# Sample attention beside GDN's chain: ScalarE copies every turned page out of PSUM, in place of taking turns with VectorE

## Chip, cores and metric

One core of a Trainium2 chip runs the whole kernel. The metric is the device time of one execution in microseconds (us); lower is better. The kernel before takes 1189.36 us in the median of three runs (1189.23 to 1190.71).

## The reference, cut to what matters

The reference is one inference step of a decoder layer for two groups that share all weights: a prompt of 16 meta tokens and 512 tokens, and a sample group of 8 sequences with 8 new tokens each. A token-mixing block runs two branches on one input projection: differential attention, and a gated DeltaNet (GDN). Then come gates, an output projection and a gated ConvFFN. The change touches the sample group's attention over its cache: each of the 8 sequences has 2048 cached keys in 16 pages of 128 tokens, found through a page table.

```python
k_past = cache_k[l][page_table].reshape(ds, -1, DA_HEADS, 2, DA_HEAD_DIM)
v_past = cache_v[l][page_table].reshape(ds, -1, DA_HEADS, 2 * DA_HEAD_DIM)
s_past = jnp.einsum('bqhmd,bkhmd->bhmqk', qs, k_past)
s_new = jnp.einsum('bqhmd,bkhmd->bhmqk', qs, k)
pr = jax.nn.softmax(jnp.concatenate([s_past, s_new], axis=-1), axis=-1)
a = pr[:, :, 0] - lam * pr[:, :, 1]
out = einsum('bhqk,bkhe->bqhe', a[..., :n_past], v_past) + einsum(..., a[..., n_past:], v)
```

GDN, which runs beside it, solves a triangular system per chunk of 128 tokens and carries a state from chunk to chunk; it does so for four heads, one after the other.

## The kernel before, in words

**Two streams.** Lines 228 to 247 merge two generators into one program. The main stream does the prompt's attention and then, from `self.chain = True` on (line 232), the four GDN heads (`gdn_chain`, line 711). The stream beside it does the sample attention (line 1353) and then 16 gate projections. While the chain flag is set the main stream has right of way, and the other stream is recorded wherever the main stream asks for a delay. A scheduler below that lays the instructions out in one fixed order on each engine when the program is built, so an edit to one operation can move others.

**Sample attention** takes the sequences in four pairs. A page of keys arrives by DMA from SP's queue as `page` (a tile holds two pages; five tiles rotate). TensorE turns it: four transposes of 128x128, one per head (line 419), into one PSUM bank `ps_t` (three banks rotate). The bank is copied into `KT` (line 1403, 128x512); then TensorE multiplies `KT` by the queries into the bank `ps_s` (one bank), from which VectorE makes the masked scores `S` and their maxima (line 1235). A `KT` tile holds two pages, j = 0 and j = 1: VectorE copies j = 0 and ScalarE copies j = 1. There are 64 `KT` tiles in all, 16 to a pair. After the softmax the pages of values are multiplied without being turned.

**GDN's chain.** Per head, three convolutions (lines 647 and 649 on VectorE, 653 on ScalarE) give q, k and v; two Gram products follow, and then a solve of the 16x16 blocks, `gdn_base` (line 936): row sums (969, 970), a first step (971), and 14 steps of shuffle, multiply and subtract (975 to 977) that run on VectorE alone, one after the other. Their end is `xyt` and `xy` (981, 987), which TensorE transposes to go on. Products that widen the solved blocks follow, and the chunk-by-chunk state (875 to 909). Between these TensorE does wide projection products into `ps_d` (for `z`, the next head's q, k and v, and gates); their weights are loaded as `wraw` (line 309), rounded by ScalarE into `whi` (313), and VectorE subtracts to get `wlo` (314).

Of the kernel before, what the change touches and what calls it, by code (L numbers as in the profile page):

```python
# [150 lines left out]
class Body:  # L151
# [1201 lines left out]
    def sample_attention(self, pool):  # L1353
        nc, a = self.nc, self.a
# [23 lines left out]
        def pages(cache, ids):  # L1378

            t = self.t(pool, [128, 2, 512], "page", bufs=5)  # L1380
            for k, i in enumerate(ids):
                tag, value = entry(cache, i)
                move = nc.sync.dma_start(t[:, k], cache[bass.ds(value, 1)].rearrange("o t e -> (o t) e"))
                moves[tag] = move.ins
            return t

        for pr in range(NB // 2):
# [4 lines left out]
            for g in range(4):  # L1392
                sp = self.ps("s")
                for u in range(2):
                    kts = []
                    for e in range(2):
                        kp = pages(ck, [(2 * pr + e) * NPG + 4 * g + 2 * u + j for j in range(2)])
                        kt = self.t(pool, [128, H, 256], "KT", bufs=4)
                        for j in range(2):
                            tp = self.ps4("t")  # L1400
                            for h in range(H):
                                self.transpose(tp[:, h], kp[:, j, 128 * h : 128 * h + 128])
                            (nc.scalar.copy if j % 2 else nc.vector.tensor_copy)(kt[:, :, 128 * j : 128 * j + 128], tp)  # L1403
                        kts.append(kt)
                    yield DELAY[26]
                    for e, kt in reversed(list(enumerate(kts))):
                        for h in range(H):
                            self.mm(
                                sp[32 * h : 32 * h + 32, 256 * u : 256 * u + 256], self.qb[:, 2 * pr + e, h], kt[:, h],
                                start=e == 1, stop=e == 0,  # L1410
                            )
                    yield 0.0
                self.score(S[:, 512 * g : 512 * g + 512], sp, self.zeros(512), -3e38, mx[:, g : g + 1])
# [16 lines left out]
            tp = self.ps("t")  # L1430
# [9 lines left out]
            for g in range(4):  # L1440
                tp = self.ps4("t")
# [24 lines left out]
            if pr % 2:  # L1466
                self.head_norm(pool, os)
                yield DELAY[30]
                tp = self.ps("t")
# [722 lines left out]
```

## Time and profile before

| | value |
|---|---|
| median of 3 runs | 1189.36 us |
| the profiled execution | 1191.39 us, of which the span from first to last instruction is 1189.6 us |
| TensorE's mean granted clock | 0.983 |
| TensorE busy | 1136.4 us, 96% |
| VectorE busy | 734.6 us, 62% |
| ScalarE busy | 512.1 us, 43% |

Times in rows are microseconds from the span's start unless they are marked ns. PE is TensorE, PEld its weight loads, DVE VectorE, ACT ScalarE, POOL GpSimd, and SPq SyncE's queue of DMA issues. An idle time in square brackets is that of the engine just before the row, with what ended it.

### The profile page before, as it was taken

Reading aid. Unit: us, or ns where it says so; the run is one execution under the profiler, and the core shown is the slowest. Engines: PE = TensorE matmul, PEld = TensorE weight load, DVE = VectorE, ACT = ScalarE, POOL = GpSimd, SP = SyncE. Lnnn points to the kernel's source line nnn. Section 1 sums busy time; section 2 is a strip of 40 time slices with the busy share of each in tenths; the row PEclk is TensorE's granted clock in tenths of the full one; section 3 lists DMA queues with packets and bytes.
Section 4 is the critical chain, followed back from the end, with each engine's and each line's share of the span. In section 5 each row is a group of like instructions: output and inputs, shape, how many; then the busy total and the mean of one; then the engine's idle time right before and its main releaser. Section 6 shows DMA issues by size and latency. Waiting matters only on the chain.

```text
span 1189.6 us, 23613 instructions
## 1 busy us (share of the span) xinstructions
PE 1136.4 (96%) x8683; PEld 1014.2 (85%) x8683; DVE 734.6 (62%) x1877; ACT 512.1 (43%) x1242; POOL 283.1 (24%) x390
## 2 busy tenths in 40 slices
PE   6999999988999998999999999999999999999997
PEld 5987787766677777779999897789999999999996
DVE  5446657578389368446333874479889889842323
ACT  5235545443253343324232534445565565832321
POOL 2122221041242223213010001434554544300000
PEclk9999999998999999999999999989999999999999
DMA  6374434835857674742323346323333332432322
GB/s 201 79 242 137 134 86 131 272 112 173 275 164 232 215 249 145 231 125 55 89 55 83 88 124 188 114 73 105 100 91 95 103 89 82 136 98 74 103 74 80
DMA packets 184348, 157.56 MB, mean 132 GB/s; under 512 B 12571, under 2 KB 146274, under 8 KB 184232
## 3 DMA queue, kind: packets, MB, share of 16 engines
q1 hardware_dynamic: 179713, 147.53, 41.2%
q0 software_dynamic: 3264, 5.16, 1.4%
q10 hardware_dynamic: 1254, 3.35, 0.9%
q8 instruction: 69, 1.13, 0.4%
q14 instruction: 48, 0.39, 0.1%
HBM read 146.12 MB, written 9.88 MB: 131 GB/s over the span
## 4 chain that ended last, share of the span: by engine, by line
PE 71%; issue 13%; DVE 8%; POOL 3%; ACT 3%; DMA 1%; SPq 0%; DVEq 0%; POOLq 0%; ACTq 0%
PE ps_d L271 26%; PE ps_t L271 17%; PE ps_g L271 14%; PE ps_s L271 6%; PE ps_t L419 6%; PE ps_m L271 1%; DVE cy L649 1%; DVE KT L1403 1%; DMA page<-in_cache_v 1%; DVE vt L656 1%; POOL grr L786 1%; POOL r L383 0%; POOL dbig_up L749 0%; POOL hss L383 0%; DMA x<-in_x_prompt 0%
## 5 line engine op out<-in xcount | busy, mean ns | idle before, releaser
L271 PE MATMUL ps_d<-xhi,whi 128*128 128x256 f32 (+2 forms) x704 | 219.8, 313 | 0.0
L314 DVE TENSOR_TENSOR wlo<-wraw,whi 128x512 fp32r<-128x512 f32 x196 | 138.4, 721 | 127.7 <-ACT whi L313 126.0
L271 PE MATMUL ps_d<-xhi,wlo 128*128 128x256 f32 (+2 forms) x704 | 213.9, 304 | 0.6 <-DVE wlo L314 0.6
L271 PE MATMUL ps_d<-xlo,whi 128*128 128x256 f32 (+2 forms) x704 | 213.9, 304 | 0.3 <-DVE xlo L314 0.2
L313 ACT CAST whi<-wraw 128x512 fp32r<-128x512 f32 (+1 forms) x198 | 117.0, 611 | 165.4 <-PE ps_d L271 94.1
L271 PEld LDWEIGHTS ps_d<-xhi,whi 128*128 128x128 f32 x704 | 134.8, 192 | 7.8 <-issue 4.6
L271 PEld LDWEIGHTS ps_d<-xlo,whi 128*128 128x128 f32 x704 | 134.8, 192 | 3.6 <-issue 2.5
L271 PEld LDWEIGHTS ps_d<-xhi,wlo 128*128 128x128 f32 x704 | 134.5, 191 | 1.9 <-DVE wlo L314 1.0
L419 PE MATMUL ps_t<-consts,page 128*128 128x128 f32 x512 | 73.5, 283 | 7.7 <-DVE KT L1403 6.5
L419 PEld LDWEIGHTS ps_t<-consts,page 128*128 128x128 f32 x512 | 57.5, 143 | 24.4 <-issue 10.3
L271 PE MATMUL ps_t<-fhit,hw 128*128 128x290 f32 x228 | 68.0, 298 | 0.0
L271 PE MATMUL ps_t<-flot,hw 128*128 128x290 f32 x228 | 67.7, 297 | 0.0
L271 PE MATMUL ps_t<-fhit,lw 128*128 128x290 f32 x228 | 67.6, 297 | 0.0
L1403 ACT COPY KT<-ps_t 128x512 f32<-128x512 f32 x64 | 37.4, 585 | 65.4 <-PE ps_t L419 63.0
L313 ACT CAST hw<-sw 128x512 fp32r<-128x512 f32 x76 | 47.2, 623 | 40.6 <-PE ps_t L271 19.8
L314 DVE TENSOR_TENSOR lw<-sw,hw 128x512 fp32r<-128x512 f32 x76 | 59.4, 782 | 8.1 <-ACT hw L313 8.1
L1403 DVE COPY KT<-ps_t 128x512 f32<-128x512 f32 x64 | 43.7, 684 | 19.0 <-PE ps_t L419 18.8
L271 PEld LDWEIGHTS ps_t<-flot,hw 128*128 128x128 f32 x228 | 43.2, 190 | 0.0
L271 PEld LDWEIGHTS ps_t<-fhit,lw 128*128 128x128 f32 x228 | 43.1, 189 | 0.0
L271 PEld LDWEIGHTS ps_t<-fhit,hw 128*128 128x128 f32 x228 | 43.0, 189 | 0.0
L271 PE MATMUL ps_s<-KT,qb 128*32 128x256 f32 x512 | 38.1, 402 | 1.4 <-DVE KT L1403 1.1
L1870 DVE SCALAR_TENSOR_TENSOR fy<-fpre,fw,fy 128x592 f32<-128x592 f32 x44 | 36.5, 828 | 0.9 <-ACT fy L1868 0.2
(683 smaller groups left out, 3073.8 us busy)
## 6 DMA issues: line engine op xcount, KB each, us to landing
page<-in_cache_k SPq DMA_DIRECT2D x128, 256.0 KB, 4.3
page<-in_cache_v SPq DMA_DIRECT2D x128, 256.0 KB, 4.5
wraw<-in_w_in SPq DMA_DIRECT2D x88, 256.0 KB, 3.0
wraw<-in_w_ffn_in SPq DMA_DIRECT2D x50, 256.0 KB, 3.0
wraw<-in_w_down SPq DMA_DIRECT2D x40, 256.0 KB, 3.5
raw<-in_w_ffn_in SPq DMA_DIRECT2D x38, 256.0 KB, 2.9
wraw<-in_w_out SPq DMA_DIRECT2D x16, 256.0 KB
x<-in_x_prompt SPq DMA_DIRECT2D x4, 512.0 KB, 8.6
```

Of the source, the lines that this page charges most:

```text
L271: return self.nc.tensor.matmul(out, lhsT, rhs, **kw).ins
L313: self.nc.scalar.copy(hi, raw)
L314: (eng or self.nc.vector).tensor_tensor(out=lo, in0=raw, in1=hi.bitcast(F32), op=ALU.subtract)
L419: self.nc.tensor.transpose(out, in_, self.ident[:k, :k])
L649: nc.vector.scalar_tensor_tensor(out=y, in0=pre[:, j : j + n], scalar=self.cw[:, ch, 24 + j : 25 + j], in1=y, op0=ALU.mult, op1=ALU.add)
L656: nc.vector.scalar_tensor_tensor(out=dst, in0=part(th), scalar=1.0, in1=part(y_), op0=ALU.add, op1=ALU.mult)
L786: nc.gpsimd.tensor_tensor(out=rr, in0=rr, in1=self.mhalf[:, :10].rearrange("p (a b) -> p a b", a=2), op=ALU.pow)
L1403: (nc.scalar.copy if j % 2 else nc.vector.tensor_copy)(kt[:, :, 128 * j : 128 * j + 128], tp)
L1870: nc.vector.scalar_tensor_tensor(out=y, in0=pre[:, j : j + 592], scalar=fw[:, m, 16 + j : 17 + j], in1=y, op0=ALU.mult, op1=ALU.add)
```

## The change

Pages that are recorded while the chain flag is set are copied by ScalarE for both j; before that the two engines go on taking turns.

```diff
                             for h in range(H):
                                 self.transpose(tp[:, h], kp[:, j, 128 * h : 128 * h + 128])
-                            (nc.scalar.copy if j % 2 else nc.vector.tensor_copy)(kt[:, :, 128 * j : 128 * j + 128], tp)
+                            copy = nc.scalar.copy if j or self.chain else nc.vector.tensor_copy
+                            copy(kt[:, :, 128 * j : 128 * j + 128], tp)
                         kts.append(kt)
```

Of the 64 copies on VectorE 42 move to ScalarE: 10 of the second pair, which is under way when the chain starts, and 16 each of the third and the fourth. A new line shifts later line numbers by one. The scheduler then lays the engines out differently from there on, in three places above all.

TensorE while it turns pages beside the first head's solve, before (`page` and `KT` are the sample group's keys, `ps_d` the wide products, here for `z`):

```order
1183 L419 MATMUL ps_t_3723<-consts_66,page_3710 128x128 x4
1184 L271 MATMUL ps_d_4435<-xhi_6_85,whi_4428 128x256
1185 L271 MATMUL ps_d_4435<-xlo_7_86,whi_4428 128x256
1186 L419 MATMUL ps_t_3729<-consts_66,page_3710 128x128 x4
1187 L271 MATMUL ps_d_4462<-xhi_8_87,whi_4428 128x322
1188 L271 MATMUL ps_d_4462<-xlo_9_88,whi_4428 128x322
1189 L419 MATMUL ps_t_3747<-consts_66,page_3743 128x128 x4
```

And the same pages now:

```order
1182 L419 MATMUL ps_t_3723<-consts_66,page_3710 128x128 x4
1183 L419 MATMUL ps_t_3729<-consts_66,page_3710 128x128 x4
1184 L419 MATMUL ps_t_3747<-consts_66,page_3743 128x128 x4
1185 L419 MATMUL ps_t_3753<-consts_66,page_3743 128x128 x2
1186 L271 MATMUL ps_s_3684<-KT_3722,qb_304 32x256 x4
```

The wide products no longer stand between the pages. From the transposes of `kn` to the transpose of `xyt` TensorE's order had 49, 44 and 44 of them in the three solves with pages beside them; now it has 15, 2 and 15, and the others stand behind `xyt`. Eight score products moved behind it as well in the second and in the third of these solves.

VectorE in the first head's solve, before:

```order
538 L971 TENSOR_TENSOR xc_3617<-xc_3617,lc_3615 128x5
539 L1403 COPY KT_3697<-ps_t_3698 128x4x128
540 L975 STREAM_SHUFFLE row_3628<-xc_3617 128x5x2
541 L1403 COPY KT_3722<-ps_t_3723 128x4x128
542 L976 TENSOR_TENSOR row_3628<-row_3628,lc_3615 128x5x2
543 L1403 COPY KT_3746<-ps_t_3747 128x4x128
544 L977 TENSOR_TENSOR xc_3617<-xc_3617,row_3628 128x5x2
```

And now:

```order
536 L971 TENSOR_TENSOR xc_3617<-xc_3617,lc_3615 128x5
537 L314 TENSOR_TENSOR wlo_4429<-wraw_4424,whi_4428 128x512
538 L975 STREAM_SHUFFLE row_3628<-xc_3617 128x5x2
539 L314 TENSOR_TENSOR wlo_4432<-wraw_4426,whi_4428 128x512
540 L976 TENSOR_TENSOR row_3628<-row_3628,lc_3615 128x5x2
541 L314 TENSOR_TENSOR wlo_4513<-wraw_4508,whi_4512 128x512
542 L977 TENSOR_TENSOR xc_3617<-xc_3617,row_3628 128x5x2
```

The page copies are gone from between the steps; the weight subtractions, which stood a few steps further on, moved up into their places.

SP's queue of loads, before, where the next head's weights `wraw_4637` to `wraw_4749` are asked for (`page` from `in_cache_v` are pages of values):

```order
298 L1383 DMA page_4018<-in_cache_v 128x512
299 L309 DMA wraw_4510<-in_w_in 128x4x128
300 L309 DMA wraw_4637<-in_w_in 128x4x128
301 L309 DMA wraw_4639<-in_w_in 128x4x128
302 L309 DMA wraw_4747<-in_w_in 128x4x128
303 L309 DMA wraw_4749<-in_w_in 128x4x128
```

And now:

```order
365 L1383 DMA page_4390<-in_cache_k 128x512
366 L720 DMA st_4499<-in_state_gdn 128x8x128
367 L309 DMA wraw_4637<-in_w_in 128x4x128
368 L309 DMA wraw_4639<-in_w_in 128x4x128
369 L309 DMA wraw_4747<-in_w_in 128x4x128
```

Those loads moved back past all pages of values of this pair, four tiles of the next pair's keys and the next head's state.

## Rows read from the trace of the kernel before

**Rows 1.** The page: busy time, share of the span, instructions.
```profile
PE 1136.4 (96%) x8683; PEld 1014.2 (85%) x8683; DVE 734.6 (62%) x1877; ACT 512.1 (43%) x1242; POOL 283.1 (24%) x390
```

**Rows 2.** Stretches: PE, PEld, DVE, ACT, POOL busy (count), PEclk, DMA share, GB/s.
```profile
255.00:265.00 10.00, 7.99 (x55) 5.45 (x54) 5.88 (x20) 3.84 (x10) 3.43 (x4) 0.83 0.08 23
265.00:275.00 10.00, 6.40 (x56) 4.90 (x54) 9.88 (x20) 2.73 (x5) 5.37 (x6) 0.88 0.61 189
275.00:285.00 10.00, 9.93 (x88) 6.66 (x86) 7.44 (x31) 2.35 (x4) 1.12 (x2) 0.78 0.56 161
```

**Rows 3.** TensorE's waits, 235 to 545 us: in total, times, longest.
```profile
PE ps_t L419 <- DVE KT L1403: 6.9, 5, 3.2
...
PE ps_t L419 <- ACT KT L1403: 2.1, 3, 1.4
...
PE ps_t L419 <- DVE tailT L639: 1.2, 1, 1.2
```

**Rows 4.** Line 1403 by engine, whole span: ns min/median/max, first and last start.
```profile
L1403 DVE COPY KT<-ps_t x64: 669/684/692, 65.1 to 475.9; 128x512 f32<-128x512 f32 x64
L1403 ACT COPY KT<-ps_t x64: 564/586/604, 65.9 to 476.2; 128x512 f32<-128x512 f32 x64
```

**Rows 5.** Line 1403 in the three solves: DVE and ACT busy (count), PEclk, DMA.
```profile
255.00:295.00 40.00, 6.83 (x10) 5.87 (x10) 0.87 0.51 153
355.00:387.00 32.00, 8.18 (x12) 7.02 (x12) 1.00 0.71 219
451.00:483.00 32.00, 6.82 (x10) 5.88 (x10) 0.95 0.64 198
```

**Rows 6.** TensorE in order of time, around the three solves: start, length, instruction, [idle].
```profile
258.21 0.29 PE L419 MATMUL ps_t<-consts,kn 80*128 80x80 f32 x1 [2.01 <-DVE kn L793]
...
274.20 1.11 PE L419 MATMUL ps_t<-consts,page 128*128 128x128 f32 x4 [3.22 <-DVE KT L1403]
...
293.41 0.27 PE L419 MATMUL ps_t<-consts,xyt 80*80 80x80 f32 x1
...
355.44 0.68 PE L419 MATMUL ps_t<-consts,kn 80*128 80x80 f32 x5
356.05 1.07 PE L271 MATMUL ps_s<-KT,qb 128*32 128x256 f32 x16
357.05 1.53 PE L419 MATMUL ps_t<-consts,page 128*128 128x128 f32 x12
...
386.02 0.27 PE L419 MATMUL ps_t<-consts,xyt 80*80 80x80 f32 x1
...
451.16 0.67 PE L419 MATMUL ps_t<-consts,kn 80*128 80x80 f32 x5
...
482.53 0.27 PE L419 MATMUL ps_t<-consts,xyt 80*80 80x80 f32 x1
```

**Rows 7.** VectorE in order of time, first solve.
```profile
262.78 0.69 DVE L1403 COPY KT<-ps_t 128x512 f32<-128x512 f32 x1 [2.27 <-PE ps_t L419]
263.39 0.85 DVE L649 SCALAR_TENSOR_TENSOR cy<-pre,cw,cy 128x616 f32<-128x616 f32 x1
...
272.71 0.83 DVE L971 TENSOR_TENSOR xc<-xc,lc 128x5 f32<-128x5 f32 x1
...
278.26 0.69 DVE L1403 COPY KT<-ps_t 128x512 f32<-128x512 f32 x1 [1.21 <-PE ps_t L419]
...
293.12 0.24 DVE L981 TENSOR_TENSOR xyt<-xc,consts 80x80 f32<-80x80 f32 x1
```

**Rows 8.** ScalarE in order of time, first solve.
```profile
275.40 0.59 ACT L1403 COPY KT<-ps_t 128x512 f32<-128x512 f32 x1 [5.13 <-PE ps_t L419]
```

**Rows 9.** Stretch with wide products alone: PE busy (count), PEclk, DMA share, GB/s.
```profile
290.00:293.00 3.00, 3.00 (x22) 1.00 1.02 298
```

**Rows 10.** What SP's queue waited for, 225 to 560 us: in total, times, longest.
```profile
SPq L720 <- DMA out_new_gdn_sample<-st: 8.6, 2, 7.0
```

**Rows 11.** The tile `wraw`, 225 to 560 us: from issue to landing.
```profile
DMA to landing us min/median/max: 3.0/3.9/4.8
```

## The prediction

> **What bounds the kernel now.** I read the page first. TensorE is busy for 96% of the span, VectorE for 62%, ScalarE for 43% [rows 1]. So what counts is TensorE's idle time and its clock; moving work between the other two engines pays only where TensorE waits for one of them. Over the whole span a VectorE with 38% to spare says nothing of that, so the next view is the table of stretches. Around the first head's solve it shows what the averages hide: from 265 to 275 us VectorE is busy for 9.88 of 10 us and TensorE for only 6.40, and ScalarE for 2.73 [rows 2]. In this stretch VectorE is the bound and ScalarE is free. The clock is part of it: the granted clock is 0.83, 0.88 and 0.78 in three slices of 10 us [rows 2], so 3.4, 2.4 and 4.4 us of them passed at 1.2 instead of 2.4 GHz, each after TensorE had waited.
>
> The list of waits says for whom. Between 235 and 545 us TensorE waits 6.9 us for page copies on VectorE, 2.1 us for those on ScalarE and 1.2 us for another late VectorE copy, `tailT` [rows 3]. The longest, 3.22 us, ends at 274.20 [rows 6]; ScalarE meanwhile had been idle for 5.13 us because no turned page came [rows 8]. The page sat in PSUM behind a queue of GDN work on VectorE. That is 10.2 us in the three rows, the size of the prize. The trace in order of time shows who is late next: the solve on VectorE runs from 272.71 to the `xyt` at 293.12 [rows 7], and TensorE takes `xyt` up at 293.41 [rows 6] at once. It had wide products to do until then.
>
> **What the change moves.** 42 copies leave VectorE, 42 x 0.684 = 28.7 us, and 42 x 0.586 = 24.6 us come to ScalarE [rows 4]. Neither sum is on TensorE's path as such. I therefore work out each of the three solves with pages beside them, from TensorE's `kn` to its `xyt`: how much earlier VectorE delivers, less the TensorE work that the new order puts off until after `xyt`. That work isn't saved, only done later, and it has to be paid from the same 96%.
>
> *First solve:* 35.2 us now, 258.21 to 293.41 [rows 6]. Ten VectorE copies leave it [rows 5], at 0.61 us from one start to the next, 262.78 to 263.39 [rows 7]: 6.1 us. Two waits of VectorE for turned pages, 2.27 and 1.21 us [rows 7], go with them, as far as nothing else (the Gram products, which TensorE does after the same pages) is late then. Bounds 6.1 and 9.6 us; I take 8.3, near the upper one, since the copy that waited 1.21 us stood inside the chain of steps, where nothing takes its place. Put off: 49 - 15 = 34 wide products. A stretch with such products alone does 22 in 3.00 us [rows 9], 0.136 us each: 4.6 us. Gain 8.3 - 4.6 = 3.7 us, between 1.5 and 5.0. TensorE itself, without its wait for copies and with part of the half clock gone, would be at `xyt` 2 to 4 us before VectorE: the wait for pages turns into a shorter wait for the solve.
>
> *Second solve:* 30.6 us now, 355.44 to 386.02 [rows 6], at full clock [rows 5]. Twelve copies go, 7.3 us; one weight subtraction moves in, about 0.6 us as any VectorE pass over 128x512. 6.7 us earlier. Put off: 44 - 2 = 42 wide products, 5.7 us, and eight score products, which are the 16 matmuls of a row of 1.07 us [rows 6]: 6.8 us. Gain 0, between -1.5 and +1.
>
> *Third solve:* 31.4 us now, 451.16 to 482.53 [rows 6]. Ten copies, 6.1 us; put off 29 x 0.136 = 3.9 and again 1.1 us. Gain 1.1, between 0 and 2.5.
>
> *Where the third and the fourth pair of sequences start,* outside of the solves: the 1.2 us for `tailT` and the longest wait for a ScalarE copy, 1.4 us [rows 3]. Both were late because VectorE was: the second stood in ScalarE's order behind a SiLU of a convolution that VectorE had not finished. Four and six VectorE copies leave there. 2.6 us; bounds 0 and 3.4.
>
> *What it costs.* A pair of pages that two engines copied side by side in 0.68 us takes ScalarE 2 x 0.586 = 1.17 us [rows 4]. TensorE needs 2 x 0.51 us to turn them (twelve transposes in 1.53 us make three pages) and half of 1.07 us for their scores [rows 6], 1.55 us together. So ScalarE keeps up on average with a quarter to spare; that is the cover, and it is gone where several pages are turned without scores between them, as the new order does more often. GDN's own small copies on ScalarE queue behind pages too. I take 1 us; bounds 0 and 10.2 (21 pairs x 0.49 us, each on the path). The Trainium skill, "TensorEngine Tiling (Array Packing)", section "PSUM Bottleneck", speaks against this change: use both ScalarE and VectorE to empty PSUM. By it the cost is the upper bound, and the sum would come out 9.2 us later; by the row, TensorE's 1.55 us hide it.
>
> *After the new waits* for `xyt` the clock may fall again, as it did after the old ones. Such a slice lost half of 4.4 us, 2.2 us [rows 2]. Two solves have such a wait; I take 1.5 us, between 0 and 4.4.
>
> *DMAs:* the next head's weight loads stand behind the pages of values, keys and the state on SP's queue. They now follow a state load that waited up to 7.0 us for a store [rows 10], and land 3.0 to 4.8 us after issue [rows 11]. In TensorE's new order 32 page transposes and 38 wide products stand between the state's last product and the first product with those weights for the next head, and 48 and 62 for the one after: at 0.51 us for four transposes [rows 6] and 0.136 us for a wide product [rows 9] that is at least 9.3 and 14.5 us. So I cost it at nothing; the cover is that work.
>
> **Sum:** 3.7 + 0 + 1.1 + 2.6 - 1.0 - 1.5 = 4.9 us less. Against the profiled execution of 1191.39 us that is 1186.5; the median of the runs is 2.03 us below that execution, so 1184.5 us.
>
> **The rivals.**
>
> *The wait only changes its name.* If the first solve gains its lower bound, the second its own, and the clock falls after each new wait, then 1.5 - 1.5 + 0 + 2.6 - 1 - 2.2 = -0.6: 1190.0 us, no change. For it: TensorE was not late for any of the three `xyt`, so it is VectorE's chain that ends these stretches, before and after. Against: VectorE's chain does lose ten to twelve copies each time.
>
> *The clock stays up.* If the waits left are too short or too scattered for the clock to fall, and the upper bounds hold: 5.0 + 1.0 + 2.5 + 2.6 = 11.1 us, 1178.3 us. For it: the second solve had only small waits and kept 1.00 throughout [rows 5]. Against: its new order leaves just two wide products to fill the time.
>
> *ScalarE becomes the bound (slower).* Every page waits in one queue, behind rounding of weights, SiLUs and softmax. If TensorE waits in every pair, 10.2 us come back in place of 1.0: 1184.5 + 9.2 = 1193.7 us. It decides from where ScalarE's queue holds a page for longer than the three `ps_t` banks cover, that is two pages ahead, about 1 us; a single activation that waits for VectorE is enough. For it: the one ScalarE wait of 1.4 us came about in that way. Against: in the solves ScalarE is busy for 2.35 to 3.84 of 10 us [rows 2], and ten copies more add 6 us to 40.
>
> *Weights late (slower).* If the state's store holds the queue for its 7.0 us in both heads and the cover is half of what I think, some 5 us twice are lost: 1194.5 us.
>
> **How the numbers follow.** A measurement of this kernel can tell about 0.2%, 2.4 us, from no change. My forecast, a gain between 2.4 and 9 us, gets 0.49; the change of name 0.21; the clock that stays up 0.13; ScalarE as the bound 0.12; late weights 0.05. Faster: 0.49 + 0.13 = 0.62. Same: 0.21. Slower: 0.17. The range runs from the upper bounds together, 1178, to 1193, which leaves out the two slow cases at their full price and anything beyond 11 us of gain, less than 2 in 10. The likeliest case's own range is 1180 to 1187.
>
> **What would show it.** Right: line 1403's successor has 106 copies on ScalarE and 22 on VectorE; TensorE's waits for VectorE's `KT` are gone after 258 us; from `kn` to `xyt` it takes about 26.9, 23.9 and 25.3 us; TensorE waits 2 to 4 us for `xyt` or for `ps_s` in the first and third solve, and the wide products stand behind it. Wrong: waits of TensorE for ScalarE's `KT` of several microseconds, or for `whi`; a `kn` to `xyt` time as long as before; or a granted clock near 0.8 after each solve.

## The result, and the profile after

The changed kernel takes 1192.34 us in the median of 15 runs (1187.31 to 1196.76), the kernel before 1189.01 us in as many beside it: a ratio of 1.0033, 95% interval 1.0017 to 1.0049. It is slower, by little, where a gain of 0.4% was forecast. The profiled execution took 1193.68 us, its span is 1191.6, against 1191.39 and 1189.6 before.

The page answers to [rows 1]: VectorE has lost 19 us of work and ScalarE won 20, and TensorE is busy for slightly less.

```profile
PE 1133.5 (95%) x8683; PEld 1014.6 (85%) x8683; DVE 715.8 (60%) x1835; ACT 532.0 (45%) x1284; POOL 287.5 (24%) x390
```

The changed line by engine, whole span (answers to [rows 4]: nanoseconds least/median/greatest, first and last start):

```profile
L1404 ACT COPY KT<-ps_t x106: 567/592/642, 66.0 to 480.8; 128x512 f32<-128x512 f32 x106
L1404 DVE COPY KT<-ps_t x22: 671/692/693, 65.3 to 242.6; 128x512 f32<-128x512 f32 x22
```

TensorE's waits from 235 to 545 us (answers to [rows 3]):

```profile
PE ps_s L271 <- DVE smx L1235: 5.2, 4, 1.4
...
PE ps_d L271 <- DVE wlo L314: 3.8, 1, 3.8
...
PE ps_t L419 <- DVE xyt L981: 1.2, 1, 1.2
...
PE ps_t L419 <- ACT KT L1404: 0.8, 1, 0.8
...
PE ps_t L419 <- DVE tailT L639: 0.5, 1, 0.5
```

The 10.2 us for `KT` on both engines and for `tailT` that made up the prize are down to 1.3. In their place stand scores that VectorE takes late (`smx`), and a single wait of 3.8 us for a weight subtraction, `wlo`. TensorE in order of time (answers to [rows 6]):

```profile
258.03 0.29 PE L419 MATMUL ps_t<-consts,kn 80*128 80x80 f32 x1 [2.01 <-DVE kn L793]
...
285.10 0.27 PE L419 MATMUL ps_t<-consts,xyt 80*80 80x80 f32 x1
...
356.94 0.67 PE L419 MATMUL ps_t<-consts,kn 80*128 80x80 f32 x5
...
381.61 0.24 PE L419 MATMUL ps_t<-consts,xyt 80*80 80x80 f32 x1 [1.18 <-DVE xyt L981]
...
434.80 0.67 PE L419 MATMUL ps_t<-consts,on 128*128 128x128 f32 x5
...
443.53 0.39 PE L271 MATMUL ps_d<-xhi,wlo 128*128 128x256 f32 x1 [3.75 <-DVE wlo L314]
...
459.47 0.67 PE L419 MATMUL ps_t<-consts,kn 80*128 80x80 f32 x5
...
485.24 0.27 PE L419 MATMUL ps_t<-consts,xyt 80*80 80x80 f32 x1
```

All three solves are shorter: 27.1, 24.7 and 25.8 us from `kn` to `xyt`, against 35.2, 30.6 and 31.4 (`kn` is a head's scaled keys; their transposes begin its solve). But the third `kn` comes 8.3 us later than before, 459.47 against 451.16 [rows 6]: between the second head's `on` (the transpose of its output, at 435.92 before) and that `kn` 15.2 us have become 24.7. The two stretches around that `on` show what happened. Before (start and end, busy of PE, PEld, VectorE, ScalarE, GpSimd with counts, granted clock, DMA share, GB/s):

```profile
425.00:435.00 10.00, 9.50 (x90) 7.33 (x89) 8.91 (x24) 4.03 (x12) 2.88 (x3) 1.00 1.00 323
435.00:445.00 10.00, 8.63 (x63) 7.52 (x62) 6.80 (x17) 7.03 (x28) 4.15 (x6) 1.00 0.48 138
```

And now:

```profile
425.00:435.00 10.00, 9.99 (x95) 8.32 (x94) 0.70 (x2) 5.27 (x10) 0.00 (x0) 1.00 0.98 292
435.00:445.00 10.00, 6.25 (x45) 4.30 (x44) 9.56 (x18) 6.29 (x19) 5.52 (x3) 0.95 0.21 71
```

VectorE did 8.91 us of work in the first stretch; now it does 0.70 there, is full in the next, and TensorE falls from 8.63 to 6.25. The work that moved, beside four page copies that ScalarE now does, is the convolution for the fourth head's keys. It runs a head ahead: the third head's keys `kt` had been written long before, and the fourth's wait until TensorE has turned those (from 436.75 on), as both use one buffer:

```profile
345.60 1.16 DVE L656 SCALAR_TENSOR_TENSOR kt<-pre,cy 128x512 f32<-128x512 f32 x3 [0.76 <-ACT pre L653]
...
449.05 0.91 DVE L656 SCALAR_TENSOR_TENSOR kt<-pre,cy 128x512 f32<-128x512 f32 x3 [2.69 <-PE ps_t L419]
```

Before, VectorE's order of time had this convolution's first copy (line 625) and its last step (649) at

```profile
428.71 0.21 DVE L625 COPY pre<-ps_d 128x64 f32<-128x64 f32 x1
...
434.40 0.89 DVE L649 SCALAR_TENSOR_TENSOR cy<-pre,cw,cy 128x616 f32<-128x616 f32 x1
```

and now VectorE stands still for 6.56 and 3.62 us first (`S` are scores, `ob` is the second head's output, which needs the transpose of `on`):

```profile
431.12 0.69 DVE L1235 CUSTOM_DVE_ANT_0 S<-ps_s,consts 128x512 f32<-128x512 f32 x1 [6.56 <-PE ps_s L271]
...
435.44 1.07 DVE L931 SCALAR_TENSOR_TENSOR ob<-ps_t,gnorm,z 128x512 f32<-128x512 f32 x3 [3.62 <-PE ps_t L419]
436.43 0.22 DVE L625 COPY pre<-ps_d 128x64 f32<-128x64 f32 x1
...
440.95 0.84 DVE L649 SCALAR_TENSOR_TENSOR cy<-pre,cw,cy 128x616 f32<-128x616 f32 x1
...
442.32 2.84 DVE L314 TENSOR_TENSOR wlo<-wraw,whi 128x512 fp32r<-128x512 f32 x2
```

The `wlo` that TensorE waits for at 443.53 stands behind that convolution. Why the convolution is late, ScalarE's copies of its two halves out of PSUM tell (lines 623 and 624). The second half came at 425.46 before:

```profile
425.46 0.37 ACT L624 COPY pre<-ps_d 128x256 f32<-128x256 f32 x1
```

and now 11.0 us after the first:

```profile
424.85 0.37 ACT L623 COPY pre<-ps_d 128x256 f32<-128x256 f32 x1 [0.83 <-PE ps_d L271]
...
435.87 0.37 ACT L624 COPY pre<-ps_d 128x256 f32<-128x256 f32 x1 [0.28 <-PE ps_d L271]
```

TensorE was at work all that time (9.99 of 10 us): its order has pages of keys between these products. Their weights had long been ready, the last `wlo` before 442.32 having been made at 370.07. Counted in the built programs, these are the wide products that TensorE has behind it at each point:

| | `xyt` 1 | `on` 1 | `kn` 2 | `xyt` 2 | `on` 2 | `kn` 3 | `xyt` 3 | `on` 3 |
|---|---|---|---|---|---|---|---|---|
| before | 961 | 1008 | 1104 | 1148 | 1221 | 1296 | 1340 | 1380 |
| changed | 927 | 1000 | 1104 | 1106 | 1198 | 1296 | 1311 | 1380 |

The 42 that were put off in the second solve are not made up by `on`: 23 still lack: the last two for the fourth head's keys, and 21 for its queries.

### The profile page after: what moved, and what is told of

Read it like the earlier page. It is cut to its first block, busy times and chain, and to the rows that moved or that the text cites. A ratio compares the mean times of both kernels' runs of the same rounds, so it can differ in the third digit from the quotient of the medians.

```text
span 1191.6 us, 23623 instructions
## 1 busy us (share of the span) xinstructions
PE 1133.5 (95%) x8683; PEld 1014.6 (85%) x8683; DVE 715.8 (60%) x1835; ACT 532.0 (45%) x1284; POOL 287.5 (24%) x390
## 4 chain that ended last, share of the span: by engine, by line
PE 70%; issue 12%; DVE 10%; POOL 3%; ACT 3%; DMA 1%; SPq 0%; DVEq 0%; POOLq 0%; ACTq 0%
PE ps_d L271 27%; PE ps_t L271 17%; PE ps_g L271 14%; PE ps_t L419 6%; PE ps_s L271 5%; DVE cy L649 1%; PE ps_m L271 1%; DVE wlo L314 1%; DMA page<-in_cache_v 1%; DVE row L976 1%; DVE row L975 1%; DVE xc L977 1%; DVE vt L656 1%; POOL r L383 0%; ACT gjunk L767 0%
## 5 line engine op out<-in xcount | busy, mean ns | idle before, releaser
L1404 ACT COPY KT<-ps_t 128x512 f32<-128x512 f32 x106 | 57.3, 597 | 43.3 <-PE ps_t L419 43.1
L419 PE MATMUL ps_t<-consts,page 128*128 128x128 f32 x512 | 70.0, 281 | 1.9 <-ACT KT L1404 0.8
L271 PE MATMUL ps_s<-page,pT 128*32 128x256 f32 x512 | 34.7, 385 | 0.8 <-DMA page<-in_cache_v 0.7
```

Of the source, the lines that this page charges most:

```text
L271: return self.nc.tensor.matmul(out, lhsT, rhs, **kw).ins
L419: self.nc.tensor.transpose(out, in_, self.ident[:k, :k])
L1404: copy(kt[:, :, 128 * j : 128 * j + 128], tp)
```

## The experiments

Each run below is compared with runs of the kernel before on the same chip; the times in the headings are ratios to it with their 95% intervals. Stretches are read from one profiled execution of each kernel, which lies up to 6.4 us from its median. The theory was that the order costs (**A**), not the copies (**B**). To part them, a table put an engine back into another kernel's order:

```diff
+PE_ORDER = (
...
+)
+def keep_order(tc, *tables):
+    ins = {i.name: i for i in tc.nc.cur_bb.bb.instructions}
...
+            tc.add_manual_dep(
+                ins[y], x, mybir.DependencyInfo(mybir.DependencyClass.NoSync, mybir.DependencyReason.DATA), reason="order"
+            )
...
         Body(tc, ctx, a, o).run()
+        keep_order(tc, PE_ORDER)
```

Each instruction `y` of the table is issued behind the one ahead of it, `x`, on its own engine; no wait on another engine is added. Engines without a table are laid out by the scheduler, so their orders can differ between the runs.

**1. Copies changed, TensorE's order of before: 0.9972 (0.9955 to 0.9988).** The table holds TensorE's order of before over all rows that the change had moved.

> The changed copies (ScalarE for all 42), with TensorE's order of before put back by a table; the other engines are laid out anew. Theory A, the order: the loss was made by TensorE's new order, which puts the products for the next head's keys behind xyt, so that VectorE's convolution starts 10 us later; without it the waits for KT (10.2 us before) go and on-to-kn of the second head takes about 15 us again, not 24.7: 1180 to 1187 us. Rival B, the copies: one engine for all pages costs by itself, whatever the order: 1191 to 1196 us, with TensorE waiting for ScalarE's KT. Rival C, nothing but names: 1188 to 1191 us.

1187.29 us: faster than before, just beyond the upper end of what A said. From `on` to `kn` of the second head it takes 13.75 us at full clock (stretches as above):

```profile
432.92:446.67 13.75, 13.75 (x99) 12.77 (x98) 8.84 (x27) 5.75 (x27) 3.42 (x5) 1.00 0.29 87
```

**2. Copies of before, TensorE's order of the change: 1.0325 (1.0310 to 1.0340).** The same edit on the kernel before, with the other table.

> The copies of before (VectorE and ScalarE in turns), with TensorE's order of the changed kernel put on by a table. Theory A, the order: slower than before although no copy is moved, 1192 to 1200 us, with 22 us or more from on to kn of the second head and VectorE idle for several us before it; the copies on VectorE make the solves as long as before on top. Rival B, the copies: as before, 1188 to 1190 us. Rival C: 1188 to 1191 us.

1229.46 us, worse than A said: no copy is moved, and it loses ten times what the change lost. From `on` to `kn` of the second head:

```profile
457.74:483.62 25.88, 20.69 (x142) 18.53 (x141) 18.01 (x45) 11.04 (x41) 9.72 (x10) 0.87 0.28 81
```

Much as in the changed kernel (24.7), and on top TensorE waits 11.1 us for `xyt`, since VectorE still copies pages in the solves while the products that filled the time stand behind it. Its granted clock from the first `kn` to the fourth is 0.91 on average.

**3. Copies changed, orders of before on TensorE, VectorE and SyncE's queue: 0.9928 (0.9906 to 0.9949).** `keep_order(tc, PE_ORDER, DVE_ORDER, SP_ORDER)`.

> The changed copies, with the order of before on TensorE, on VectorE (less the 42 copies) and on SyncE's queue. Theory A, the order: like the run with TensorE's order alone, 1180 to 1187 us. If that run is slow and this one fast, it is VectorE's or the queue's order that costs. Rival B, the copies: 1191 to 1196 us. Rival C: 1188 to 1191 us.

1182.55 us: this version beats both kernels. The copies alone, with these three orders kept, are worth what was forecast and more; B is refuted. The second head's `on` to `kn`, and what is left of the waits for `KT` (235 to 560 us):

```profile
429.08:443.57 14.49, 14.05 (x99) 12.77 (x98) 9.47 (x26) 6.77 (x29) 3.93 (x6) 1.00 0.23 70
```

```profile
PE ps_t L419 <- ACT KT L1404: 1.9, 3, 1.0
...
PE ps_s L271 <- ACT KT L1404: 0.8, 1, 0.8
```

**4. Only the fourth pair's 16 copies moved: 0.9989 (0.9971 to 1.0006).**

```diff
-copy = nc.scalar.copy if j or self.chain else nc.vector.tensor_copy
+copy = nc.scalar.copy if j or (self.chain and pr == 3) else nc.vector.tensor_copy
```

> ScalarE copies all pages of the fourth pair alone (16 copies moved, not 42). In the changed kernel the stretch from the third kn to the fourth was 5.9 us shorter than before and the two before it were 1.7 and 6.8 us longer. Theory A, the order: the fourth pair's gain stays and the losses go: 1183 to 1187 us. Rival B, the copies: about 1190 us (16 of 42 parts of the loss). Rival C: the 5.9 us were work that had been done earlier, at the second head's expense: 1188 to 1191 us.

1188.96 us, no difference that this can tell: A's 1183 to 1187 was missed. The profiled execution (1184.38 us at a clock of 0.991) has A's step: 95.2 us from the third `kn` to the fourth in place of 100.2. The median, at 0.987, does not bear it out.

**5. The order split: the solves as changed, what follows as before: 0.9959 (0.9946 to 0.9972).** Copies changed; the table is the changed kernel's TensorE order, in which the rows from each `xyt` to the next `kn` are sorted as they stood before.

> The changed copies, with TensorE's order of the changed kernel from kn to xyt in each of the three solves, and the order of before for what then follows up to the next kn. Theory A1, products late: the loss lies behind xyt, where 23 wide products for the next head's keys stand behind on; so from on to kn the second head takes 13 to 16 us again, not 24.7, the solves stay short (27, 25 and 26 us), and the time is 1183 to 1188 us. Theory A2, the solves: what costs is the pages close together with the wide products put off until after xyt: 1190 to 1195 us, with TensorE idle in the solves as in the changed kernel.

1186.35 us. The solves stay at 27.0, 24.9 and 24.6 us, and the second head's `on` to `kn` takes

```profile
433.28:448.26 14.98, 14.98 (x116) 13.08 (x114) 9.50 (x29) 6.83 (x30) 3.69 (x6) 1.00 0.21 61
```

TensorE is never idle there. The waits for `smx` are the changed kernel's (5.3 us): they are not what costs.

**6. The reverse: the solves as before, what follows as changed: 1.0134 (1.0112 to 1.0155).**

> The reverse: the changed copies, TensorE's order of before from kn to xyt, and the relative order of the changed kernel from xyt to the next kn. Theory A1, products late: 18 us or more from on to kn of the second head, and 1189 to 1195 us. Theory A2, the solves: 1183 to 1188 us.

1205.84 us, beyond the expected range. The same place, 26 us and a lower clock:

```profile
436.32:462.42 26.10, 19.31 (x127) 18.28 (x125) 18.15 (x45) 10.83 (x41) 9.44 (x10) 0.87 0.28 77
```

It differs from run 1 in TensorE's table between `xyt` and `kn` alone, and by 1.6%. With the order of before behind `xyt` the ratio is 0.9972 or 0.9959 (runs 1 and 5, solves as before and as changed), with the changed order 1.0134 or 1.0033 (this run and the changed kernel). The loss sits behind `xyt`, not in the solves.

**7. As run 3, SyncE's queue free: 0.9951 (0.9938 to 0.9963).** `keep_order(tc, PE_ORDER, DVE_ORDER)`.

> The changed copies with the orders of before on TensorE and VectorE, SyncE's queue laid out anew. With all three orders of before the time was 1182.55 us, with TensorE's alone 1187.29. Theory V, VectorE's order makes the difference (TensorE waits in the solves because scores and weight subtractions stand in the wrong place between the steps): 1181 to 1185 us. Theory Q, the queue of loads makes it: 1185.5 to 1189 us.

1185.51 us, just inside Q's range and just outside V's, which decides nothing: its interval overlaps those of runs 1 and 3 (its profiled execution took 1191.88 us, so no stretch is read from it). VectorE's order and the queue's together make the difference between runs 1 and 3; how it divides is not settled.

**8. All orders of before, half of the copies moved (`e == 1`): 0.9992 (0.9977 to 1.0007).** `j or (self.chain and e == 1)`, with tables as in run 3.

> All orders of before, and only 21 of the 42 copies moved: of the two KT tiles of a group one goes to ScalarE whole, the other is still shared, so ScalarE copies three pages of four. Rule of two engines: a mix empties PSUM better than one engine, 1178 to 1182 us, faster than with all 42 moved (1182.55). Rival, VectorE is what ends the solves: half of the gain, 1185 to 1188 us.

1190.53 us: neither. Half of the copies give nothing that this can tell. TensorE waits in the same three places as before, for the copies that stayed:

```profile
271.86 1.12 PE L419 MATMUL ps_t<-consts,page 128*128 128x128 f32 x4 [3.35 <-DVE KT L1404]
...
455.61 1.11 PE L419 MATMUL ps_t<-consts,page 128*128 128x128 f32 x4 [2.35 <-DVE KT L1404]
...
464.82 0.66 PE L419 MATMUL ps_t<-consts,page 128*128 128x128 f32 x4 [1.27 <-DVE KT L1404]
```

Before, these waits were 3.22 [rows 6], 2.35 and 0.55 us, the second here:

```profile
456.93 1.11 PE L419 MATMUL ps_t<-consts,page 128*128 128x128 f32 x4 [2.35 <-DVE KT L1403]
```

**9. Copies changed, only the queue's order of before: 1.0195 (1.0158 to 1.0231).** `keep_order(tc, SP_ORDER)`.

> The changed copies, with the order of before on SyncE's queue alone (the next head's weight loads stand ahead of the pages of values again); the compute engines are laid out anew, and TensorE then has 1272 wide products behind it at the second head's on, where before had 1221 and the changed kernel 1198. Theory L: the place of the weight loads in the queue is what put the products late; with them early, on to kn of the second head takes 9 to 14 us, and the time is 1181 to 1187 us. Rival P: what fills the wait for xyt matters more than what precedes on; with 51 more wide products ahead of on the state's chain is later by as much, 1188 to 1193 us.

1213.12 us. Theory L falls, and P was too mild. From `on` to `kn` it is short, as L said (11.5 and 12.5 us in the first two heads), but the state's steps ahead of `on` have swelled from 28.0 to 42.2 us in the first head:

```profile
304.20:346.38 42.18, 39.29 (x331) 30.16 (x329) 19.96 (x54) 15.47 (x48) 14.10 (x11) 1.00 0.73 254
```

With early loads the scheduler sets products ahead of the state's steps, and they cost there what they no longer cost behind `on`: all that follows the first two `xyt` takes 72.3 and 76.4 us, about as in the changed kernel (71.8 and 77.9). What makes this run slower still lies behind the third `xyt`, 82.3 us in place of 68.5, of which TensorE stands idle for 11.6:

```profile
486.93:569.21 82.28, 70.69 (x571) 56.96 (x571) 29.24 (x76) 26.25 (x78) 16.43 (x14) 0.94 0.46 134
```

Its longest wait there, 4.6 us, is for `oS`, a result of the sample attention on VectorE. No run settles what the loads have to do with that.

**10. The changed kernel with one stretch of TensorE's order put back, `xyt` 2 to `kn` 3: 0.9985 (0.9967 to 1.0002).**

> The changed kernel with TensorE's order of before in one stretch alone, from the second head's xyt to the third kn (solves and the other heads stay as changed). In the run with all three such stretches the second one gave back 9.7 us from on to kn and paid 5.3 us of it after xyt; the first gave 3.7 us from on to kn and 2.9 us before it. Theory A1: some 4 to 7 us less than the changed kernel, 1185 to 1188.5 us against 1191 for before; from on to kn 14 to 16 us. Rival: the first head's stretch carries it, and this one stays within 2 us of the changed kernel: 1190 to 1194 us.

1189.61 us; by the ratios 0.48%, 5.7 us, below the changed kernel, the difference that A1 named, and not the rival's 2 us; the time itself lies 1.1 us above A1's range. From `on` to `kn`, in a profiled execution of 1195.82 us:

```profile
440.51:455.50 14.99, 14.99 (x115) 13.08 (x113) 9.28 (x27) 6.84 (x30) 3.69 (x6) 1.00 0.20 56
```

That one stretch holds about two thirds of what run 5 gives back (0.74%), by the medians; the intervals are about 0.2% wide to each side.

**11. Copies changed, only VectorE's order of before: 1.0115 (1.0091 to 1.0140).** `keep_order(tc, DVE_ORDER)`.

> The changed copies with VectorE's order of before alone (less the 42 copies); TensorE, ScalarE and the queue are laid out anew, and TensorE's order then has 958, 1149 and 1344 wide products behind it at the three xyt, nearly as before (961, 1148, 1340), and 1026 and 1224 at the first two on. Theory A1: since the products are where they were, 1182 to 1187 us, as with the orders of TensorE and VectorE put back. Rival: details of TensorE's order other than the place of the wide products decide: 1189 to 1194 us.

1204.98 us: missed. From `on` to `kn` of the second head it takes 14.29 us, and at `kn` 3 the kernel is 1.0 us ahead of before; then the third solve takes 40.1 us. TensorE waits there for rounded weights,

```profile
478.94 0.58 PE L271 MATMUL ps_d<-xhi,whi 128*128 128x256 f32 x1 [5.14 <-ACT whi L313]
```

whose loads SyncE's queue issues from 473.11 on, behind ten loads of pages of values (the queue in order of time):

```profile
465.50 7.51 SPq L1383 DMA_DIRECT2D page<-in_cache_v  x10
473.11 6.89 SPq L309 DMA_DIRECT2D wraw<-in_w_in  x4
```

After that wait the granted clock falls, in the solve and most of all behind it:

```profile
450.14:490.24 40.10, 29.16 (x268) 22.04 (x265) 23.75 (x96) 18.27 (x34) 7.91 (x10) 0.90 0.51 159
490.24:510.10 19.86, 19.52 (x135) 14.63 (x135) 4.82 (x10) 4.27 (x12) 1.37 (x2) 0.59 0.38 118
```

0.10 of 40.1 and 0.41 of 19.9 us make 12 us lost to the lower level; before lost 5 us to it from its third `kn` to the third `on`. This is the rival "weights late" of the prediction, in another kernel. That this place alone makes the run slow is read from its trace; it wasn't tried.

**12. As run 8, the other half (`e == 0`): 0.9988 (0.9972 to 1.0004).**

> All orders of before, and the other 21 copies moved: of the two KT tiles of a group the one that is turned first goes to ScalarE whole, the second is still shared. When the second tile's copies were moved, TensorE still waited 3.35, 2.35 and 1.27 us for VectorE's KT, in the same three places as before (3.22, 2.35, 0.55); all three are copies of the first tile. Theory place: it counts which copies stand behind GDN's work in VectorE's queue, not how many; these waits go, and the time comes near that of all 42 (0.9928 of before): 0.992 to 0.996. Rival number: half of the copies give half of the gain or, as the other half did, nothing: 0.997 to 1.000.

1187.95 us: the theory of places falls too. The waits have moved one step on, from the next page to the score:

```profile
274.33 1.07 PE L271 MATMUL ps_s<-KT,qb 128*32 128x256 f32 x16 [3.25 <-DVE KT L1404]
...
461.68 1.07 PE L271 MATMUL ps_s<-KT,qb 128*32 128x256 f32 x16 [2.03 <-DVE KT L1404]
```

A group's scores need both tiles. One copy left in VectorE's queue holds them about as long as two.

## Why the prediction was wrong, point by point

The profiled executions, cut at TensorE's `kn` and `xyt` (us, from rows as above; a head's solve, and all that follows it up to the next `kn`):

| | solve: forecast | measured | behind `xyt`: forecast | measured |
|---|---|---|---|---|
| head 1 | -8.3 | -8.1 | +4.6 | +9.8 |
| head 2 | -6.7 | -5.9 | +6.8 | +12.7 |
| head 3 | -6.1 | -5.6 | +5.0 | -0.3 |
| sum | -21.1 | -19.6 | +16.4 | +22.2 |

**The solves were right.** How much earlier VectorE delivers `xyt` was priced at 21.1 us and came out at 19.6: 27.1, 24.7 and 25.8 us stand beside the forecast 26.9, 23.9 and 25.3. The waits for VectorE's `KT` are gone.

**The step that failed is "Put off".** "That work isn't saved, only done later, and it has to be paid from the same 96%": it was priced as TensorE's time alone, so many products by 0.136 us, wherever they land. That time was about right. Behind the second `xyt` run 5 does the same 190 wide products as the changed kernel, 115 of them ahead of `on` in place of 92. Run 5 takes 72.9 us from that `xyt` to the next `kn`, 7.8 more than before against the 6.8 priced; the changed kernel takes 77.9 (first row the changed kernel, second run 5):

```profile
381.61:459.47 77.86, 72.49 (x632) 57.44 (x633) 32.54 (x87) 29.73 (x86) 19.57 (x19) 0.98 0.64 204
375.34:448.26 72.92, 71.01 (x633) 55.62 (x633) 32.62 (x87) 29.30 (x87) 17.62 (x18) 1.00 0.64 207
```

The other 4.9 us come from the place of the products: TensorE is idle for 5.4 us in place of 1.9, and the clock is 0.98 in place of 1.00. Runs 1 and 6 say the same with nothing put off: 148 products behind that `xyt` in both, 65.9 and 77.7 us. The products have a reader, the convolution for the fourth head's keys, some 6 us on VectorE from its first copy to its last step. No `kn` before the fourth needs it. But each engine has one order, and in VectorE's order the third head's `kn` and the next `wlo` stand behind it. Before, it ran while TensorE was still turning pages ahead of `on`. Put off, its last products came after the pages, VectorE stood still for 10.2 us, and the convolution moved out of its cover onto the path: TensorE had to wait for the `wlo` behind it. In the changed kernel and in runs 2 and 6 its first copy (line 625) starts 1.6 to 1.8 us behind the second `on`, and from `on` to `kn` it takes 24.7 to 26.1 us; in the other eleven kernels it starts some 7 us or more ahead, and it takes 12.5 to 15.2. Runs 5 and 6 show that TensorE's order behind `xyt` carries the loss, run 10 that the second head's stretch holds most of it; runs 1 and 3 that without it the copies gain. In the third head nothing is late, since all 1380 products are made by `on` 3 in either order, and that head gains 5.9 us in all.

**The clock** was priced at 1.5 us after the new waits, in the first and third solve. It fell after the first solve and around the two `on`:

```profile
285.10:334.62 49.52, 47.31 (x412) 36.77 (x411) 13.96 (x46) 18.21 (x47) 9.71 (x10) 0.93 0.65 206
334.62:356.94 22.32, 19.94 (x130) 18.66 (x131) 18.42 (x49) 9.92 (x38) 10.13 (x12) 0.92 0.50 155
```

That is 3.5 and 1.8 us, and 1.7 in the second head: 7.0 us, where the bound was 4.4. In the first head the 5.3 us are as much as the excess over the forecast 4.6; with the order of run 5 the clock is 1.00 from the first `xyt` to the second `kn`, which takes 65.3 us, 3.3 more than before. Against it stand 8.6 us that the clock gave back elsewhere: it is 0.94 in the first solve (0.85 before) and 1.00 from the third `kn` to the third `on` (0.95 and 0.92 before, in the solve and after it). Part of that may be chance: the profiled execution of before had a mean of 0.983, where the median of its runs in the experiments was 0.986. By the medians the clock is the same in both kernels, 0.986 and 0.987, and what is left as the loss is TensorE's idle time, 23.4 us from the first `kn` to the fourth in place of 18.7.

**Where the pairs start,** 2.6 us were expected from two waits; one is gone and `tailT` is down from 1.2 to 0.5 us, but both lie in the stretches that grew. (The table leaves out the sum's terms 2.6, 1.0 and 1.5; together they come to -0.1 us.) **What it costs on ScalarE** was put at 1.0 us and is 0.8 (2.7 in run 3). The rival "ScalarE becomes the bound" is refuted by run 3: all pages in ScalarE's queue, and faster than before. The Trainium skill, "TensorEngine Tiling (Array Packing)", section "PSUM Bottleneck", would have both engines empty PSUM; the runs disagree here, where one of the two also carries the chain: mixes gave 0.9992 and 0.9988, one engine 0.9928.

**Weights late** was not it either: TensorE waited for no `whi`, and run 9, with the loads where they had been, is slower still. **The wait only changes its name** comes near in time but not in mechanism: it took no account of a convolution behind `xyt`. So the prediction asked who is late next inside of each solve, and stopped there; the slower side was sought on ScalarE and the queue, while it lay in what the products were for.

**What stays open:** how the gain from run 1 to run 3 divides between VectorE's order and the queue, and which of the scheduler's choices put the products behind the pages. That neither the queue's nor VectorE's order alone brings it back, runs 9 and 11 show. Nor was the changed kernel run with the third head's `kn` and the `wlo` alone put ahead of the convolution on VectorE: that the path leads over it is read from the traces.

## What to carry to other kernels

Where a scheduler lays a program out anew, an edit is two changes, the operation and the order; put the old order back to see what each is worth, as here -0.7% and +1.0%. When filler work is put off, price not only its own time but ask who reads it, what stands behind that reader on its engine, and whether the reader's work still has its cover. And a bottleneck copy is not halved by moving half of it, if the half that stays sits in the same queue and the same consumer needs both.

## What the hardware showed besides

Two subtractions `wlo`, 0.69 us each at the median, took 1.15 and 1.77 us from 442.32 on, while GpSimd was busy on operands in SBUF:

```profile
442.32 1.15 DVE L314 TENSOR_TENSOR wlo<-wraw,whi 128x512 fp32r<-128x512 f32 x1
```

```profile
440.90 2.02 POOL L749 TENSOR_TENSOR dbig_up<-dd,consts 128x512 f32<-128x512 f32 x1
442.89 1.73 POOL L813 TENSOR_TENSOR er<-q,er 128x512 f32<-128x512 f32 x1
```

Each of them ended 0.55 us after the GpSimd instruction that was under way when it began. TensorE waited for the first, so some 0.5 of its 3.75 us came from there. The Trainium skill, "SBUF — State Buffer", section "SBUF: two separate sides", has VectorE and GpSimd share a pair of ports that an instruction with two SBUF inputs holds or waits for as a whole; the trace agrees in this place. VectorE's copy from PSUM beside the first of them (line 765) took its usual 0.68 us.

Times of one kernel go with the granted clock: the changed kernel's 15 range from 1187.31 us at a mean of 0.992 to 1196.76 us at 0.983. That spread of 0.8% is over twice the effect measured, so the interval, not a pair of runs, decides here.
